# A hybrid diffusion trunk on one core: the first output group of each feed-forward chunk accumulates in four PSUM banks, and six modulation groups of TensorE stand at other places

## The chip, the cores and the metric

One NeuronCore of a Trainium2 chip runs the whole step as one program. The metric is the device time of that program in microseconds (us), the median of repeated executions; lower is better.

## The reference, cut to what matters

Two layers work on 640 tokens (512 latent, 128 context) of width 1024, in float32. Each layer is rmsnorm and half-step SwiGLU, rmsnorm and token mixing, rmsnorm and half-step SwiGLU. The norms are modulated by vectors that come from a conditioning vector through a wide matrix (`ada_w`).

```python
mod = (jax.nn.silu(cond) @ ada_w[i] + ada_b[i]).reshape(-1, N_MOD, D_MODEL)
h = modulate(rms_norm(x, norm_g[i, 0]), mod[:, 0], mod[:, 1])
x = x + 0.5 * mod[:, 2] * swiglu(h, ffn_w_in[i, 0], ffn_w_out[i, 0])
...
def swiglu(h, w_in, w_out):
    g, u = jnp.split(h @ w_in, 2, axis=-1)
    return (jax.nn.silu(g) * u) @ w_out          # inner width 2816 = 22 x 128
```

There are four feed-forward blocks, called F1 to F4 here (layer 0 first and last, layer 1 first and last).

## The kernel before, in words

**Layout.** Activations lie transposed: a tile is 128 channels by 640 tokens, and `x` is eight of them. A matmul takes a 128x128 weight tile as its stationary operand and half of the tokens, 320 columns, as its moving operand; `hf` names the half. Each float32 product is three matmuls of rounded operands (`mm3x`, lines 695 to 697): high by high, high weight by low activation, low weight by high activation. So every weight and every activation is split into a high part (a copy on ScalarE, `whi`, line 308) and a low part (a subtraction on VectorE, `wlo`, line 309).

**A feed-forward block.** Its 22 inner tiles are made in chunks of 6, 8 and 8 (`CHUNKS`), called c1, c2 and c3. For each inner tile `strassen_in` runs seven products into the three PSUM banks `pu`, `pg` and `pf`; ScalarE and VectorE then form the activation tile, first its high part (line 890), then its low part (line 891). Inner tiles are numbered 0 to 21; the trace names them `a`, layer, block, number (`a005h` is the high part of tile 5 of F1). After a chunk `out_proj` adds the chunk's share of the output to `x`: four weight groups (`fout`) of two output tiles, each for both token halves. One such output tile and half is a step (`op_step`): 3 matmuls for each inner tile of the chunk, in the order of the inner tiles, into one bank `op`; then VectorE adds the bank to `x` (`x_update`, line 807). The four groups of a chunk are called its section below. In c3 the x-update and the sums for the next norm have a raised priority (`tc.high_priority`), and its groups 2 and 3 run once for each half.

**Modulation groups.** Each group of 256 modulation channels (`ada`) is one load of 1 MB. Some run on TensorE (`ada`, line 447, into one bank `adaps` that is kept over four groups), the others as four long multiply-and-sum instructions on VectorE (`ada_v`, lines 404 and 406). In F1, F2 and F3 one VectorE group follows every `fout` group in the order of loads, and `mid_ada` starts it after the first step of that `fout` group. Twelve TensorE groups, six in F2 and six in F3, stand ahead of the inner tiles that `FA` lists.

**What sets the order.** All weights, `fout`, input weights and modulation groups alike, pass through a ring of two 1 MB slots (`raw`), in one written order (`order`), on SyncE's DMA queue. A weight's slot is free when its pieces are split, a modulation group's when its work is done. At most five split pieces are held; `splitter` splits ahead. TensorE's order in the feed-forward blocks and SyncE's order are those of the program text; VectorE's and ScalarE's are arranged by the compiler's scheduler, from priorities in the order of the text, and are then fixed. PSUM has eight banks (`psm`).

Of the kernel before, what the change touches and what calls it, by code (L numbers as in the profile page):

```python
# [32 lines left out]
SEGS = (((0, HT, 0),), ((HT, TL, 0), (TL, T, 1)))  # L33
NS = 47
NG0 = 2
FA = (4, 6, 9, 12, 14, 18)
QD_ = 512
NW = (6, 9)
HP = 60
# [28 lines left out]
def trunk_kernel(  # L68
# [55 lines left out]
    def stmp(name, dt=F32):  # L124
        return ap_.tile([P, T], dt, tag="s", bufs=NS, name=name)
# [5 lines left out]
    def psm(name):  # L131
        return pp.tile([P, 512], F32, tag="b", bufs=8, name=name)
# [18 lines left out]
    def spawn(gen, wait=0):  # L151
        e = [gen, wait]
        bgs.append(e)
        return e
# [57 lines left out]
    def ada_groups(l, mods):  # L212
        return [("ada", l, m * 4 + j) for m in mods for j in range(4)]

    def ffn_order(l, s):
        r, b = [], 0
        for ci, n in enumerate(CHUNKS):
            r += [("fin", l, s, g) for g in range(b, b + n)]
            r += [("fout", l, s, ci, g) for g in range(4)]
            b += n  # L220
        return r

    def weave(ws, ads, pads=(), fins=()):
        r, ads, pads = [], list(ads), list(pads)
        for w in ws:
            if pads and w[0] == "fin" and w[3] in fins:
                r.append(pads.pop(0))
            r.append(w)
            if ads and w[0] != "fin" and not (w[0] == "ein" and w[1] < 2):
                r.append(ads.pop(0))  # L230
        assert not ads and not pads
        return r

    order = [("ada", 0, m * 4 + j) for j in range(4) for m in (1, 0)]
    w00 = ffn_order(0, 0)
    q = 2 + sum(c in "ab" for c in SQ[:SQ.index("W")])
    order = order[:2] + w00[:1] + order[2:q] + w00[1:2] + order[q:]
    l1, pl = ada_groups(1, range(6)), ada_groups(1, range(6, 9))
    order += weave(w00[2:], ada_groups(0, [3, 4, 5]), ada_groups(0, [2]), (2, 3, 4, 5))
    order += weave([("ein", g) for g in range(10)] + [("eout", g) for g in range(4)], ada_groups(0, [6, 7, 8]))  # L240
    order += weave(ffn_order(0, 1), l1[:12], pl[:6], FA)
    order += weave(ffn_order(1, 0), l1[12:], pl[6:], FA)
    order += [("oin", g) for g in OORD] + [("oout", c, g) for c in range(2) for g in range(2)]
# [128 lines left out]
    def next_ada():  # L372
        if adae[0] is not None:
            finish(adae[0])
        k = order[st["i"]]
        adae[0] = spawn((ada_v if k[1:] in ADV else ada)(k))
        step(adae[0])

    def mid_ada():
        if st["i"] < nord and order[st["i"]][0] == "ada" and order[st["i"]][1:] in ADV:  # L380
            next_ada()

    def next_group(key):
        while order[st["i"]][0] == "ada":
            next_ada()
        j = st["i"]
        assert order[j] == key, (order[j], key)
        st["i"] += 1
        return Wt(j)
# [124 lines left out]
    def norm_acc(i, hf, k):  # L514
        t0, t1 = HALVES[hf]
        n = t1 - t0
        if (i, hf) not in nacc:
            acc = stmp(f"nq{i}{hf}")
            nacc[i, hf] = acc
            S.activation(out=acc[:, :n], in_=x[k][:, t0:t1], func=AF.Square)  # L520
        else:
            acc = nacc[i, hf]
            q = stmp(f"nq{i}{hf}{k}")
            S.activation(out=q[:, :n], in_=x[k][:, t0:t1], func=AF.Square)  # L524
            if k == KD - 1 and i == len(PHASES):
                nlast[i, hf] = q
            else:
                V.tensor_tensor(out=acc[:, :n], in0=acc[:, :n], in1=q[:, :n], op=ALU.add)  # L528
# [153 lines left out]

    def mm3(o, W, mcol, k, act, hf, start, stop):
        wh, wl = W.col(k, mcol)
        mm3x(o, wh, wl, *halves(act, hf), start, stop)

    def halves(act, hf):
        if len(act) == 2:
            t0, t1 = HALVES[hf]
            return act[0][:, t0:t1], act[1][:, t0:t1]  # L690
        return act[2 * hf], act[2 * hf + 1]

    def mm3x(o, wh, wl, xh, xl, start, stop, more=False):
        o = o[:, 0:HT]
        PE.matmul(o, wh, xh, start=start, stop=False, skip_group_check=more)  # L695
        PE.matmul(o, wh, xl, start=False, stop=False, skip_group_check=more)  # L696
        PE.matmul(o, wl, xh, start=False, stop=stop, skip_group_check=more)  # L697
        tick()

    def mm_fm(o, W, mcol, acts, hf, ks=None):  # L700
        ks = list(range(len(acts))) if ks is None else ks
        for i, k in enumerate(ks):
            mm3(o, W, mcol, k, acts[k], hf, i == 0, i == len(ks) - 1)

    def first_wide(i, keys, names):
# [6 lines left out]

        def go(a, k, W, hfs):
            for hf in hfs:
                for j in range(2):
                    mm3(ps[a, j, hf], W, j, k, h[k], hf, k == 0, k == KD - 1)
# [87 lines left out]
    def x_update(ps, m, l, gmod, hf):  # L804
        t0 = HALVES[hf][0]
        for a, b, c in SEGS[hf]:
            V.scalar_tensor_tensor(out=x[m][:, a:b], in0=ps[:, a - t0:b - t0],  # L807
                                   scalar=mod[:, l, gmod * KD + m, c:c + 1], in1=x[m][:, a:b],
                                   op0=ALU.mult, op1=ALU.add)

    def out_proj(keys, acts, l, gmod, nxt, ks=None):
        nw = len(keys) if nxt is None else 2
        for gi in range(nw):
            W = next_group(keys[gi])
            for j in range(2):
                for hf in range(2):
                    op_step(keys[gi], W, gi, j, hf, acts, l, gmod, nxt, ks)
                    mid_ada()
            W.done()
        if nw == len(keys):  # L820
            return
        la[0] = 2
        Ws = {}
        end = nxt == len(PHASES)
        for n_, hf in enumerate((1, 0) if end else (0, 1)):
            pe_manual((n_ == 1 or keys[0][0] == "fout") and not end)
            for gi in (2, 3):
                if n_ == 0:
                    Ws[gi] = next_group(keys[gi])
                for j in range(2):  # L830
                    op_step(keys[gi], Ws[gi], gi, j, hf, acts, l, gmod, nxt, ks)
                    mid_ada()
                if n_ == 1:
                    Ws[gi].done()
            chains[nxt, hf] = spawn(norm_chain(nxt, hf, NW[hf]))

    def op_step(key, W, gi, j, hf, acts, l, gmod, nxt, ks):
        ps = psm("op" + "_".join(str(v) for v in key[1:]) + f"_{j}{hf}")
        mm_fm(ps, W, j, acts, hf, ks)
        if nxt is None:  # L840
            x_update(ps, 2 * gi + j, l, gmod, hf)
        else:
            with tc.high_priority(HP):
                x_update(ps, 2 * gi + j, l, gmod, hf)
                norm_acc(nxt, hf, 2 * gi + j)

    def strassen_in(i, l, s, g, e):
        ahi, alo, sg = e
# [654 lines left out]
    ps = psm("n0p")  # L1503
# [4 lines left out]
    m = tiny([P, 5], "n0m")  # L1508
# [147 lines left out]
```

## Time and profile before

| | us |
|---|---|
| median of 3 runs | 2505.2 |
| lowest, highest | 2503.99, 2509.65 |
| the profiled execution, its own time | 2501.56 |
| its span in the profile | 2499.8 |

TensorE's mean granted clock over the span is 0.982 of full speed. The profiled execution lies a little below the runs; 1.8 us of it lie outside of the span.

### The profile page before, as it was taken

How to read it: one execution, taken by the hardware profiler on the slowest of the kernel's cores; microseconds unless marked ns; L12 is line 12 of the kernel's file. 1: busy time of each engine (PE TensorE's matmuls, PEld its weight loads, DVE VectorE, ACT ScalarE, POOL GpSimd, SP SyncE). 2: the span in 40 equal slices, each digit the busy share in tenths (PEclk: the TensorE clock that was granted, in tenths of full speed). 3: DMA queues.
4: the chain of work that ended last, by engine and by line, in shares of the span. 5: the costliest groups of instructions: out<-in, count | busy, mean ns of one | idle time of the engine just before them, and what ended most of it. 6: DMA issues, size and time to landing. Idle time of an engine off the chain costs nothing.

```text
span 2499.8 us, 40660 instructions
## 1 busy us (share of the span) xinstructions
PE 2398.9 (96%) x16482; PEld 2341.4 (94%) x16482; DVE 1863.5 (75%) x3785; ACT 1077.8 (43%) x2038; POOL 62.6 (3%) x86
## 2 busy tenths in 40 slices
PE   7899999999899999999999999999999998999998
PEld 6899999899898999999988999999999988999998
DVE  7677767877878777677967786789788877574674
ACT  4525335333326335153542433526767645252452
POOL 1000000000000000000000000001011000000000
PEclk9999999999999999999999999999999999999999
DMA  7342423323241333423224242342111101222121
GB/s 265 114 156 85 150 70 116 135 104 131 71 150 53 129 122 122 152 101 119 85 93 144 102 169 88 116 163 80 41 43 57 54 34 60 76 85 101 68 102 42
DMA packets 44475, 259.30 MB, mean 104 GB/s; under 512 B 5888, under 2 KB 8576, under 8 KB 16768
## 3 DMA queue, kind: packets, MB, share of 16 engines
q1 hardware_dynamic: 41024, 252.37, 28.4%
q8 instruction: 129, 2.11, 0.3%
q0 software_dynamic: 1280, 2.62, 0.3%
q10 hardware_dynamic: 1984, 1.72, 0.2%
q14 instruction: 58, 0.48, 0.1%
HBM read 252.76 MB, written 3.93 MB: 103 GB/s over the span
## 4 chain that ended last, share of the span: by engine, by line
PE 79%; DVE 11%; ACT 3%; DMA 3%; issue 2%; POOL 0%; POOLq 0%; ACTq 0%; DVEq 0%
PE op L696 7%; PE op L697 7%; PE op L695 7%; PE pu L695 7%; PE pu L696 7%; PE pu L697 7%; PE pg L697 4%; PE pg L696 4%; PE pg L695 3%; DVE wlo L309 3%; PE pf L695 2%; PE pf L696 2%; PE pf L697 2%; ACT whi L308 2%; DMA raw<-in_w_fout 1%
## 5 line engine op out<-in xcount | busy, mean ns | idle before, releaser
L309 DVE TENSOR_TENSOR wlo<-raw,whi 128x1024 fp32r<-128x1024 f32 (+1 forms) x488 | 536.1, 1116 | 282.5 <-ACT whi L308 281.4
L308 ACT ACTIVATE whi<-raw 128x1024 fp32r<-128x1024 f32 (+1 forms) x492 | 471.0, 974 | 632.5 <-DMA raw<-in_w_fout 147.8
L807 DVE SCALAR_TENSOR_TENSOR xs<-op,mod,xs 128x128 f32<-128x128 f32 (+2 forms) x312 | 127.1, 436 | 136.9 <-PE op L697 136.5
L524 ACT ACTIVATE nq<-xs 128x320 f32<-128x320 f32 x84 | 39.1, 468 | 132.2 <-DVE xs L807 130.6
L404 DVE SCALAR_TENSOR_TENSOR raw<-raw,sb 128x1024 f32<-128x1024 f32 x72 | 87.6, 1222 | 0.5
L406 DVE CUSTOM_DVE_ANT_0 raw<-raw,sb 128x1024 f32<-128x1024 f32 x72 | 87.5, 1219 | 0.7
L695 PE MATMUL oq<-H4h,whi 128*128 128x320 f32 x256 | 81.1, 318 | 0.2 <-ACT ov L967 0.2
L697 PE MATMUL oq<-H4h,wlo 128*128 128x320 f32 x256 | 79.6, 311 | 0.0
L696 PE MATMUL oq<-H4l,whi 128*128 128x320 f32 x256 | 79.3, 310 | 0.0
L1304 DVE TENSOR_REDUCE amx<-as 128x1 f32<-128x320 f32 x144 | 61.6, 461 | 19.1 <-PE as L1300 18.8
L1312 ACT ACTIVATE ap<-as,anm 128x320 f32<-128x320 f32 x128 | 66.1, 530 | 14.1 <-DVE anm L1307 13.9
L871 ACT COPY p<-pg 128x320 f32<-128x320 f32 x80 | 34.1, 426 | 64.0 <-PE pg L697 63.9
L291 DVE TENSOR_TENSOR raw<-raw 128x512 f32<-128x512 f32 x80 | 55.2, 690 | 1.9
L289 DVE TENSOR_TENSOR raw<-raw 128x512 f32<-128x512 f32 x80 | 55.2, 689 | 1.8
L290 DVE TENSOR_TENSOR raw<-raw 128x512 f32<-128x512 f32 x80 | 54.8, 685 | 0.8
L292 DVE TENSOR_TENSOR raw<-raw 128x512 f32<-128x512 f32 x80 | 54.8, 685 | 0.6
L695 PEld LDWEIGHTS oq<-H4h,whi 128*128 128x128 f32 x256 | 48.1, 188 | 1.3 <-ACT ov L967 0.5
L696 PEld LDWEIGHTS oq<-H4l,whi 128*128 128x128 f32 x256 | 48.1, 188 | 0.4 <-DVE H4l L614 0.3
L697 PEld LDWEIGHTS oq<-H4h,wlo 128*128 128x128 f32 x256 | 48.1, 188 | 0.0
L528 DVE TENSOR_TENSOR nq<-nq,nq 128x320 f32<-128x320 f32 x82 | 40.1, 491 | 9.6 <-ACT nq L524 9.1
L696 PE MATMUL pf<-H3p,whi 128*128 128x320 f32 x144 | 45.4, 316 | 1.8 <-DVE H3p L614 1.8
L696 PE MATMUL pf<-H5p,whi 128*128 128x320 f32 x144 | 44.8, 311 | 2.0 <-DVE H5p L614 2.0
(2715 smaller groups left out, 8899.2 us busy)
## 6 DMA issues: line engine op xcount, KB each, us to landing
raw<-in_w_fin SPq DMA_DIRECT2D x88, 1024.0 KB, 4.7
raw<-in_ada_w SPq DMA_DIRECT2D x64, 1024.0 KB, 4.7
raw<-in_w_fout SPq DMA_DIRECT2D x32, 1024.0 KB, 4.8
raw<-in_w_fout SPq DMA_DIRECT2D x16, 768.0 KB, 4.1
raw<-in_w_oin SPq DMA_DIRECT2D x12, 1024.0 KB, 4.8
raw<-in_w_ein SPq DMA_DIRECT2D x10, 1024.0 KB, 4.9
raw<-in_ada_w SPq DMA_DIRECT2D x32, 256.0 KB, 6.9
raw<-in_w_eout SPq DMA_DIRECT2D x4, 1024.0 KB, 4.9
```

The source lines that it names most:

```text
L289: sub.tensor_tensor(out=a22, in0=a21, in1=a22, op=ALU.add)
L291: sub.tensor_tensor(out=a11, in0=a22, in1=a11, op=ALU.subtract)
L308: S.activation(out=hf, in_=t, func=AF.Copy)
L309: sub.tensor_tensor(out=lf, in0=t, in1=hf.bitcast(F32), op=ALU.subtract)
L404: V.scalar_tensor_tensor(out=o, in0=w, scalar=1.0, in1=sb[:, c * D:(c + 1) * D], op0=ALU.mult, op1=ALU.mult, accum_out=r)
L406: V.tensor_tensor_reduce(out=o, in0=w, in1=sb[:, c * D:(c + 1) * D], scale=1.0, scalar=0.0, op0=ALU.mult, op1=ALU.add, accum_out=r)
L695: PE.matmul(o, wh, xh, start=start, stop=False, skip_group_check=more)
L696: PE.matmul(o, wh, xl, start=False, stop=False, skip_group_check=more)
L697: PE.matmul(o, wl, xh, start=False, stop=stop, skip_group_check=more)
L807: V.scalar_tensor_tensor(out=x[m][:, a:b], in0=ps[:, a - t0:b - t0], scalar=mod[:, l, gmod * KD + m, c:c + 1], in1=x[m][:, a:b], op0=ALU.m ...
L1304: V.tensor_reduce(out=mx[:, j, a:a + 1], in_=sps[j][a][:, 0:w], axis=AX.X, op=ALU.max, negate=True)
L1312: S.activation(out=pj[j][:, a * 320:a * 320 + w], in_=sps[j][a][:, 0:w], func=AF.Exp, bias=b, accum_out=(sm[:, j, a:a + 1] if full else s2 ...
```

## The change

Two edits. `FA` becomes (4, 8, 10, 12, 16, 18): of the six inner tiles that a TensorE modulation group precedes, tile 6 becomes 8, 9 becomes 10 and 14 becomes 16. And the first `fout` group of every chunk goes through the new function `op_wide` in place of four calls of `op_step`: it opens four banks, one for each output tile and half, and goes through the inner tiles in three cuts: all but the last two for each of the four banks, then the last but one for each of the four, then the last for each of the four with the x-update after each. `mid_ada` is called once, after the second cut. The x-update part of `op_step` becomes a function, `op_end`.

```diff
-FA = (4, 6, 9, 12, 14, 18)
+FA = (4, 8, 10, 12, 16, 18)
...
             W = next_group(keys[gi])
+            if gi == 0 and keys[0][0] == "fout":
+                op_wide(keys[0], W, acts, l, gmod, nxt)
+                continue
             for j in range(2):
                 for hf in range(2):
                     op_step(keys[gi], W, gi, j, hf, acts, l, gmod, nxt, ks)
                     mid_ada()
...
+    def op_wide(key, W, acts, l, gmod, nxt):
+        n = len(acts)
+        cuts = ((0, n - 2), (n - 2, n - 1), (n - 1, n))
+        jh = [(j, hf) for j in range(2) for hf in range(2)]
+        ps = {}
+        for c, (a, b) in enumerate(cuts):
+            for j, hf in jh:
+                if c == 0:
+                    ps[j, hf] = psm("op" + "_".join(str(v) for v in key[1:]) + f"_{j}{hf}")
+                for k in range(a, b):
+                    mm3(ps[j, hf], W, j, k, acts[k], hf, k == 0, k == n - 1)
+                if c == 2:
+                    op_end(ps[j, hf], j, hf, l, gmod, nxt)
+            if c == 1:
+                mid_ada()
+        W.done()
+
     def op_step(key, W, gi, j, hf, acts, l, gmod, nxt, ks):
         ps = psm("op" + "_".join(str(v) for v in key[1:]) + f"_{j}{hf}")
         mm_fm(ps, W, j, acts, hf, ks)
+        op_end(ps, 2 * gi + j, hf, l, gmod, nxt)
+
+    def op_end(ps, m, hf, l, gmod, nxt):
         if nxt is None:
-            x_update(ps, 2 * gi + j, l, gmod, hf)
+            x_update(ps, m, l, gmod, hf)
         else:
             with tc.high_priority(HP):
-                x_update(ps, 2 * gi + j, l, gmod, hf)
-                norm_acc(nxt, hf, 2 * gi + j)
+                x_update(ps, m, l, gmod, hf)
+                norm_acc(nxt, hf, m)
```

## Rows read from the trace of the kernel before

**Rows 1.** The page's first part: busy time, share of the span and number of instructions of each engine.

```profile
PE 2398.9 (96%) x16482; PEld 2341.4 (94%) x16482; DVE 1863.5 (75%) x3785; ACT 1077.8 (43%) x2038; POOL 62.6 (3%) x86
```

**Rows 2.** The timeline of TensorE at the end of the first step of F1's c1 (start in us, duration, engine, line, what is written from what; in brackets the idle time before and what ended it).

```profile
136.34 0.31 PE L697 MATMUL op<-a004h,wlo 128*128 128x320 f32 x1
137.63 0.41 PE L695 MATMUL op<-a005h,whi 128*128 128x320 f32 x1 [0.98 <-ACT a005h L890]
...
138.74 0.30 PE L697 MATMUL op<-a005h,wlo 128*128 128x320 f32 x1
```

**Rows 3.** The waits of TensorE over the whole span for parts of inner tiles: who waited for whom, idle us in total, times, longest.

```profile
PE op L695 <- ACT a105h L890: 1.4, 1, 1.4
PE op L696 <- DVE a0013l L891: 1.1, 1, 1.1
PE op L696 <- DVE a0021l L891: 1.1, 1, 1.1
...
PE op L696 <- DVE a0121l L891: 1.1, 1, 1.1
PE op L695 <- ACT a0013h L890: 1.1, 1, 1.1
PE op L696 <- DVE a1013l L891: 1.1, 1, 1.1
...
PE op L695 <- ACT a015h L890: 1.0, 1, 1.0
...
PE op L696 <- DVE a0113l L891: 1.0, 1, 1.0
PE op L696 <- DVE a1021l L891: 1.0, 1, 1.0
PE op L695 <- ACT a005h L890: 1.0, 1, 1.0
...
PE op L696 <- DVE a015l L891: 0.4, 1, 0.4
PE op L696 <- DVE a105l L891: 0.4, 1, 0.4
PE op L696 <- DVE a005l L891: 0.4, 1, 0.4
```

**Rows 4.** Stretches of the span: from and to in us, length, then busy us and number of instructions of PE, PEld, DVE, ACT and POOL, TensorE's granted clock as a share of full speed, share of the DMA engines' time, GB/s. The first follows the wait of F2's c1, the second lies behind that section of F3, the third is in the input projection of the odd layer.

```profile
848.30:851.70 3.40, 3.40 (x15) 3.40 (x14) 3.37 (x8) 0.00 (x0) 0.00 (x0) 0.50 0.30 125
...
1360.30:1367.10 6.80, 6.38 (x23) 5.94 (x24) 4.07 (x6) 2.33 (x4) 0.00 (x0) 0.50 0.44 154
...
1686.00:1692.00 6.00, 5.98 (x43) 5.72 (x42) 5.42 (x24) 3.07 (x5) 0.00 (x0) 1.00 0.37 156
```

**Rows 5.** The timeline of TensorE where F2's and F3's c2 begins, at inner tile 6: the modulation group's matmuls (`adaps`), then the products `pu`, `pg` and `pu` again, twelve matmuls each.

```profile
889.00 1.07 PE L447 MATMUL adaps<-raw,sc 128*32 128x256 f32 x16
890.00 0.41 PE L695 MATMUL pu<-H2p,whi 128*128 128x320 f32 x1
...
894.63 0.42 PE L695 MATMUL pg<-T20ah,whi 128*128 128x320 f32 x1 [2.62 <-ACT whi L308]
...
895.89 0.50 PE L697 MATMUL pg<-T20ah,wlo 128*128 128x320 f32 x1 [0.70 <-DVE wlo L309]
...
898.59 0.47 PE L695 MATMUL pu<-T20bh,whi 128*128 128x320 f32 x1
...
1355.44 0.42 PE L695 MATMUL pu<-H3p,whi 128*128 128x320 f32 x1
...
1364.45 0.47 PE L695 MATMUL pu<-T30bh,whi 128*128 128x320 f32 x1
```

**Rows 6.** The loads and splits behind that, from the timelines of SyncE's queue, ScalarE, VectorE and TensorE: first in F1, where no TensorE modulation group stands ahead of tile 6, then in F2, last the queue in F3.

```profile
162.52 0.33 SPq L267 DMA_DIRECT2D raw<-in_w_fin  x1
...
169.72 1.58 ACT L308 ACTIVATE whi<-raw 128x1024 fp32r<-128x1024 f32 x2 [10.34 <-DMA raw<-in_w_fin]
...
179.28 3.49 DVE L309 TENSOR_TENSOR wlo<-raw,whi 128x1024 fp32r<-128x1024 f32 x3
...
180.55 0.41 PE L697 MATMUL pg<-T00ah,wlo 128*128 128x320 f32 x1
...
872.95 0.33 SPq L264 DMA_DIRECT2D raw<-in_ada_w  x1
...
882.90 0.33 SPq L267 DMA_DIRECT2D raw<-in_w_fin  x1
...
887.75 1.58 ACT L308 ACTIVATE whi<-raw 128x1024 fp32r<-128x1024 f32 x2 [17.96 <-DMA raw<-in_w_fin]
...
1338.39 0.33 SPq L264 DMA_DIRECT2D raw<-in_ada_w  x1
```

**Rows 7.** Timelines in the sections: the first instruction of the second VectorE modulation group in F2's c2 and in F2's c3; in F2's c3 the first low piece of the last `fout` group, and the matmul that needs it; in F1's c3 the matmul that needs the last `fout` group.

```profile
1005.62 1.23 DVE L406 CUSTOM_DVE_ANT_0 adaj<-raw,sb 128x1024 bf16<-128x1024 f32 x1
...
1176.08 1.21 DVE L406 CUSTOM_DVE_ANT_0 adaj<-raw,sb 128x1024 bf16<-128x1024 f32 x1
...
1188.04 1.22 DVE L309 TENSOR_TENSOR wlo<-raw,whi 128x1024 fp32r<-128x1024 f32 x1 [0.68 <-ACT whi L308]
...
1192.49 0.31 PE L695 MATMUL op<-a0114h,whi 128*128 128x320 f32 x1
...
474.09 0.41 PE L695 MATMUL op<-a0014h,whi 128*128 128x320 f32 x1 [2.57 <-ACT whi L308]
```

## Prediction, made before the changed kernel ran

> **What bounds the kernel now.** I read the page's first part first [rows 1]: TensorE is busy for 2398.9 of 2499.8 us. In an engine so full only its idle time and its clock can be won by a change of order, so the views that matter are those of its waits and of its granted clock; VectorE, busy for 75%, is second and feeds it. Next, the waits of TensorE, kept to those that the two edits touch, and one of them in the timeline, to learn what a wait really costs. In F1's c1 the last matmul ahead of the wait starts at 136.34 and the third after it at 138.74 [rows 2]. A matmul follows the one before by 0.147 us when nothing is late (twelve take 1.76), so these three steps should take 0.44 and took 2.40: 1.96 lost, where the view shows 1.0 + 0.4 idle [rows 3]. Each such wait costs its idle time and some 0.27 more, in which the pipe drains and fills. Then the granted clock by stretches: behind the wait of F2's c1 it is 0.50, the lower of its two levels (1.2 of 2.4 GHz), for 3.4 us [rows 4], which costs 1.7 us more; behind F1's, as long, it did not fall. Last, what the late operand waited for, followed back through ScalarE, VectorE and the load queue [rows 6].
>
> **Part 1: the wide first group.** It removes no matmul and adds none. What it moves is the place at which the chunk's last tile is needed. The section of F1's c1 begins 14 matmuls before 136.34, at 134.29, and its first step wants tile 5 after 15 matmuls, 2.2 us; the low part is there by about 138.4. With four banks, 48 matmuls come before the last tile but one and 60 before the last: 7.0 and 8.8 us (10.5 and 12.3 in c2 and c3). So the parts, late by 2 us now, would be early by 4 or more, and I see nothing that would hold a tile back so long: its instructions stand ahead of the section's other work in the text. What this is worth, from [rows 3] with 0.27 for each wait:
> - c1: F1 1.0 + 0.4 + 0.54 = 2.0; F2 the same and 1.7 for the clock = 3.6; F3 1.4 + 0.4 + 0.54 = 2.4.
> - c2: F1 1.1 + 1.1 + 0.54 = 2.7; F2 1.0 + 0.27 = 1.3; F3 1.1 + 0.27 = 1.4.
> - c3: 1.4, 1.4 and 1.3.
> - F4 has no VectorE modulation groups in its sections and hardly waits: nothing.
>
> That is 17.5 us at the most. Bank pressure costs nothing: four banks, the last tile's three and `adaps` are eight, and the three are read before the last tile exists, so they are free long before group 1 asks for a bank. The four x-updates now come together; VectorE has the time of group 1's first step, 2.6 us or more, before anything else of TensorE's ends.
>
> Interleaving banks is something the kernel does already: the input projections change bank after every three matmuls. In one such stretch the granted clock is 1.00 and TensorE has no gap [rows 4], so I cost it at nothing. The Trainium skill ("TensorE: Matmul & The Clock Gate", section "A second HAM failure mode: psum-queue depth-cycling") says otherwise for a kernel that cycles its PSUM queue through banks: TensorE idles a little at each group of matmuls, and its clock swings between the two levels. By it the forecast would become rival 4's time; by the row it stays.
>
> **Part 2: `FA`.** A TensorE modulation group ahead of tile 6 takes a ring slot between the last modulation group of c1's section and tile 6's weights. In F2 that slot is filled at 872.95, and tile 6's own load starts only at 882.90, when the VectorE group ahead has finished; it lands at 887.7 [rows 6], and `pg`, the first product that needs the combined weights, waits for high part and low part. From 890.00 to 898.59 TensorE does 24 matmuls, 3.5 us of work, so 5.1 us are lost, and the clock is still low for some time: 5.4. In F3, 1355.44 to 1364.45, it is 5.5, and the clock stays at 0.50 to 1367.10 [rows 4, 5], 1.1 more after what two transposes rightly take: 6.6. With the group moved to tile 8, tile 6 gets the slot of 872.95. The moved group's own matmuls (1.0 us, row of 889.00) are paid at 8 instead: no change. I cost 9 to 10, 14 to 16 and 8 itself at nothing: in mid-chunk the load has a whole tile's time (84 matmuls, 12.3 us), and the present places 9, 12 and 18 show no wait. Without that cover 8 would cost what 6 does.
>
> **What is late next.** Both edits take time out of TensorE's side, and then the loads and VectorE set the pace. This is the working that cuts 29.5 us (17.5 and 12.0) down.
> - *F1, c1.* No TensorE group stands ahead of tile 6 there, and still its combined low piece is ready at 179.28 + 1.2 = 180.5 and its matmul starts at 180.55 [rows 6]: just in time, at a pace with 2.0 us of waiting in it. The chain behind (splits, modulation groups, loads) starts with the section and doesn't wait for TensorE. So most of the 2.0 comes back as a wait here: 0.5 gained, bounds 0 and 2.0.
> - *F2, c1.* TensorE would begin tile 6 at 890.00 - 1.0 - 3.6 = 885.4 and want the combined piece 14 matmuls later, at 887.5. A load issued a little behind another takes 7.2 us (162.52 to 169.72), so tile 6 lands at 880.1. From landing to that piece it takes 10.8 us in F1 (to 180.5), with a VectorE group between, and 8.1 in F2 (887.75 to 895.89); the mean, 9.4, gives 889.5. Wait: 2.0, and 0.7 for two chances in five that the clock falls. Gain 3.6 + 5.4 - 2.7 = 6.3, bounds 4 and 9.
> - *F3, c1.* By the same steps: wanted at 1355.44 - 1.0 - 2.4 + 2.05 = 1354.1, ready at 1338.39 + 7.2 + 9.4 = 1355.0. Gain 2.4 + 6.6 - 0.9 - 0.7 = 7.4, bounds 5 and 9.
> - *c2.* The next chunk's first pieces are split long ahead and held by the limit of five. I keep 5.0 of 5.4.
> - *c3.* `mid_ada` now stands after 84 of group 0's 96 matmuls instead of after 24, some 8.8 us later. Behind the waiting VectorE group in the queue are the loads of `fout` groups 2 and 3. In c1 and c2 the scheduler pulls modulation groups far ahead of their place in the text (F2's c2 starts the second one 8.4 us into its section), but in c3 it doesn't (1176.08, 20.1 us into it) [rows 7]. There a later start is really later. Slack of the last `fout` group in F2: its first low piece ends at 1189.3, it is wanted at 1192.49: 3.2 us, of which the removed wait takes 1.4. In F1's c3 there is none: TensorE waits already at 474.09, so nothing of its 1.4 is won and any delay is lost. Bounds: all 4.1 won, or a wait of F1's kind new in each: 2.57 + 0.27, less what is won, and a fall of the clock, some 4 each, so -12. I take -2.5, nearer the gain, since the slack covers most of the delay: F1 -1.5, F2 and F3 -0.5 each.
>
> Sum: 0.5 + 6.3 + 7.4 + 5.0 - 2.5 = **16.7 us**. The span goes from 2499.8 to 2483.1, the profiled execution from 2501.56 to 2484.9. That execution was 3.6 us under the median; against the median it is 2505.2 - 16.7 = **2488.5 us**.
>
> **Rivals.**
> 1. *Everything is won.* VectorE, with no x-updates during the first 8.8 us of a section, does its modulation groups sooner and nothing is given back: 29.5 us, 2475.7. For it: the idle VectorE there. Against: F1's tile 6, just in time.
> 2. *c3 is late.* The three third sections end at -12: 16.7 - 9.5 = 7.2 gained, 2498.0. For it: 1176.08 and 474.09 [rows 7].
> 3. *The other side: every section is late.* If VectorE keeps the modulation groups where the text has them in all nine sections, `fout` groups 2 and 3 come late in each, at the 2.84 of 474.09 and 1.7 for the clock, 4.5: 19.2 (the sum without c3) less 40.5 is 21.3 lost, 2526.5. It decides from 2.1 us a section on. Against it: 1005.62, far ahead of the text.
> 4. *The clock swings while banks alternate.* 24 matmuls of the second and third cut in 12 sections at 0.267 instead of 0.147 us are 34.6 us: 2523.1. Against it: the third of [rows 4]. The skill's rule named above is this one; no trace here bears it out so far.
> 5. *The wait is moved, not removed.* Tile 8 becomes what tile 6 was: the 12.0 of `FA` stay, 4.7 gained, 2500.5. Against: places 9 and 12.
>
> **How the numbers follow.** Forecast 0.58 (its own range 2481 to 2495, the bounds of c1 and c3 partly set against each other), rival 1 0.13, rival 2 0.15, rival 3 0.05, rival 4 0.02, rival 5 0.07. About 0.2%, 5 us, is what a measurement can tell from no change. Faster are the forecast, rival 1 and most of rival 2: 0.82. Same are rival 5 and the rest of rival 2: 0.11. Slower are rivals 3 and 4: 0.07. The range goes from rival 1 to the far end of rival 2, 2475 to 2503; it leaves out rivals 3 and 4 and about half of the spread around rival 1, some 0.14.
>
> **What would show it.** Right: no wait of `op` for a last tile in F1 to F3; `adaps` at tile 8, and tile 6's load about 10 us earlier in F2 and F3; waits of 0 to 3 us at the first `pg` of tile 6 in all three; no fall of the clock in c1's section of F2. Wrong: new waits of `op` for weights (`whi`, `wlo`) in groups 2 and 3, first in c3; waits at tile 8; a granted clock of 0.50 in the first groups; VectorE starting the first modulation group 12 us into a section of c1 or c2.

## The result, and the profile after

The changed kernel takes 2489.4 us (median, 2488.8 to 2490.2) against 2504.6 us (2501.8 to 2509.7) for the kernel before: a ratio of 0.9939, 95% interval 0.9926 to 0.9953, 15.2 us. A second measurement of it (experiment 5) gave 0.9924 (0.9905 to 0.9942). The forecast was 2488.5 us. Of the changed kernel there are two profiled executions, spans 2487.7 and 2488.6 us, 12.1 and 11.2 less than before. They are called the first and the second trace here; that they differ inside is a main result below.

The page's first part (first trace), which answers to [rows 1]:

```profile
PE 2395.3 (96%) x16482; PEld 2339.5 (94%) x16482; DVE 1858.1 (75%) x3785; ACT 1076.8 (43%) x2038; POOL 63.0 (3%) x86
```

TensorE's waits, first trace (who waited for whom, idle us in total, times, longest; over the whole span, so waits in stages without an edit are in the totals). The waits for inner tiles of [rows 3] are gone; what is left of `op`, `pu` and `pg` waits for weights or for a bank that ScalarE or VectorE has to read:

```profile
PE pg L697 <- DVE wlo L309: 10.3, 8, 2.7
PE pg L695 <- ACT whi L308: 9.3, 6, 2.4
...
PE op L695 <- ACT whi L308: 3.4, 2, 3.2
```

Where those behind the two edits stand, in TensorE's timeline (first trace): tile 6 of F1, the last `fout` group but one of F1's c3, tile 6 of F2, tile 6 of F3, then tiles 8 and 15 of F3. In brackets the idle time and its releaser:

```profile
179.64 0.42 PE L695 MATMUL pg<-T00ah,whi 128*128 128x320 f32 x1 [1.47 <-ACT whi L308]
...
180.90 0.41 PE L697 MATMUL pg<-T00ah,wlo 128*128 128x320 f32 x1 [0.70 <-DVE wlo L309]
...
465.43 0.64 PE L695 MATMUL op<-a0014h,whi 128*128 128x320 f32 x1 [3.18 <-ACT whi L308]
...
888.76 0.42 PE L695 MATMUL pg<-T20ah,whi 128*128 128x320 f32 x1 [1.47 <-ACT whi L308]
...
890.02 0.42 PE L697 MATMUL pg<-T20ah,wlo 128*128 128x320 f32 x1 [0.70 <-DVE wlo L309]
...
1347.61 0.41 PE L695 MATMUL pg<-T30ah,whi 128*128 128x320 f32 x1 [2.43 <-ACT whi L308]
...
1348.87 0.64 PE L697 MATMUL pg<-T30ah,wlo 128*128 128x320 f32 x1 [0.71 <-DVE wlo L309]
...
1383.66 0.42 PE L695 MATMUL pu<-T30ah,whi 128*128 128x320 f32 x1 [2.00 <-ACT a108s L897]
...
1534.24 0.41 PE L695 MATMUL pu<-T30bh,whi 128*128 128x320 f32 x1 [1.30 <-DVE p L904]
```

Windows of the first trace (columns as in [rows 4]): the wide group of F2's c1, first cut and then the cuts that alternate between four banks every three matmuls; the stretch behind the waits of F1's tile 6; the one behind 465.43.

```profile
843.00:850.00 7.00, 7.00 (x49) 7.00 (x49) 5.83 (x9) 1.95 (x4) 0.00 (x0) 1.00 0.41 150
850.00:853.60 3.60, 3.60 (x27) 3.60 (x26) 3.54 (x7) 0.00 (x0) 0.00 (x0) 1.00 0.02 5
...
181.40:184.80 3.40, 3.40 (x15) 3.40 (x14) 1.72 (x2) 0.51 (x2) 0.00 (x0) 0.50 0.53 159
...
464.70:471.60 6.90, 5.81 (x20) 5.41 (x21) 2.82 (x5) 1.62 (x2) 0.00 (x0) 0.51 0.84 292
```

The granted clock is 1.00 through the wide group and TensorE has no gap in it. So rival 4 is out: the clock doesn't swing while the banks alternate. The section of the Trainium skill that the prediction named for it ("TensorE: Matmul & The Clock Gate", "A second HAM failure mode: psum-queue depth-cycling") describes another kernel's case; this trace doesn't show it.

The span term by term. Each is measured from the start of a section to the start of the next stage that the prediction charged it to (the c1 terms from the start of c1's section to that of c2's, and so on; the c3 terms cover the section alone, and F4's holds its first chunk and the end of the span); + is time won:

```
term                     predicted   first trace   second trace
F1 c1                       +0.5        -2.2          -0.7
F2 c1                       +6.3        +5.9          +5.0
F3 c1                       +7.4        +1.3          +5.8
c2 (F1, F2, F3)             +5.0        +3.4          +5.0
c3 (F1, F2, F3)             -2.5        +1.4          -0.6
F4, sections and chunks      0          +1.3          +0.4
stages without an edit       0          +1.0          -3.7
sum                        +16.7       +12.1         +11.2
```

### The profile page after: what moved, and what is told of

It is laid out like the page before. It is cut to its first block, busy times and chain, and to the rows that moved or that the text cites. A ratio compares the mean times of both kernels' runs of the same rounds, so it can differ in the third digit from the quotient of the medians.

```text
span 2487.7 us, 40652 instructions
## 1 busy us (share of the span) xinstructions
PE 2395.3 (96%) x16482; PEld 2339.5 (94%) x16482; DVE 1858.1 (75%) x3785; ACT 1076.8 (43%) x2038; POOL 63.0 (3%) x86
## 4 chain that ended last, share of the span: by engine, by line
PE 80%; DVE 11%; ACT 3%; DMA 2%; issue 2%; POOL 0%; POOLq 0%; ACTq 0%; DVEq 0%
PE op L695 8%; PE op L697 8%; PE op L696 8%; PE pu L695 7%; PE pu L696 7%; PE pu L697 7%; PE pg L697 4%; PE pg L696 4%; PE pg L695 3%; DVE wlo L309 3%; PE pf L695 2%; PE pf L696 2%; PE pf L697 2%; PE oq L695 1%; PE atb L1378 1%
## 5 line engine op out<-in xcount | busy, mean ns | idle before, releaser
L1327 DVE TENSOR_REDUCE amx<-as 128x1 f32<-128x320 f32 x144 | 61.5, 460 | 19.1 <-PE as L1323 18.8
L1335 ACT ACTIVATE ap<-as,anm 128x320 f32<-128x320 f32 x128 | 66.2, 531 | 14.1 <-DVE anm L1330 13.9
L696 PE MATMUL pf<-H2p,whi 128*128 128x320 f32 x144 | 44.6, 311 | 1.8 <-DVE H2p L614 1.8
```

The source lines that it names most:

```text
L1327: V.tensor_reduce(out=mx[:, j, a:a + 1], in_=sps[j][a][:, 0:w], axis=AX.X, op=ALU.max, negate=True)
L1335: S.activation(out=pj[j][:, a * 320:a * 320 + w], in_=sps[j][a][:, 0:w], func=AF.Exp, bias=b, accum_out=(sm[:, j, a:a + 1] if full else s2 ...
```

## The experiments

All were timed against the kernel before, runs of one group on the same chip (1 to 4, 5 to 8, 9 to 12). Diffs are against the changed kernel.

**1 and 2. Each edit alone.** The wide group with the old `FA`, and the new `FA` with the old first group:

```diff
-FA = (4, 8, 10, 12, 16, 18)
+FA = (4, 6, 9, 12, 14, 18)
```
```diff
-            if gi == 0 and keys[0][0] == "fout":
-                op_wide(keys[0], W, acts, l, gmod, nxt)
-                continue
```

> The wide first group with the old FA. Theory A (the chain of loads and splits behind a first section starts with that section and does not wait for TensorE, so time won in c1 comes back as a longer wait at tile 6 as long as a TensorE modulation group stands there): c1 gives nothing in F2 and F3 and loses 2 in F1; c2 gives 4 to 5 us, c3 of F2 and F3 2.7, c3 of F1 loses 1.3. Together 4 to 5 us faster than before, about 2500; the wait of pg at tile 6 grows from 2.6 to 4 us or more of idle time in F2. Rival B (each edit takes away its own waits, and the two add up): 3.6 and 2.4 more are kept, about 10 us faster than before, about 2494.5, and tile 6 waits as before.

> The new FA with the old first group. Theory A: TensorE comes to tile 6 later by what it still waits for (3.6 us in F2, 2.4 in F3), the pieces are ready by then, so nearly all of 5.4 and 6.6 us is won, less up to 4 us if the new waits at tiles 8 and 15 of F3 come with FA: 8 to 12 us faster than before, 2493 to 2497; at tile 6 of F2 and F3 hardly any wait. Rival B (adding up): 15.2 less what the wide group alone gives, some 5 us faster, about 2500.

Measured: wide group alone 2490.4 us, ratio 0.9942 (0.9930 to 0.9955); new places alone 2490.7, 0.9945 (0.9932 to 0.9958). Both are better than either theory said, and the two gains, 13.9 and 13.6, don't add to 15.2. The stages that were expected do behave as theory A has it. With the wide group alone F2's c1 wins 1.4 of 3.6 and F3's 0.5 of 2.4 (in the second profile of this kernel, experiment 11, they lose 1.8 and 0.1), since TensorE, earlier at tile 6, now waits there twice (timeline of that kernel):

```profile
889.03 0.42 PE L695 MATMUL pu<-H2p,whi 128*128 128x320 f32 x1 [2.12 <-ACT whi L308]
...
890.29 0.42 PE L697 MATMUL pu<-H2p,wlo 128*128 128x320 f32 x1 [0.70 <-DVE wlo L309]
...
894.22 0.64 PE L695 MATMUL pg<-T20ah,whi 128*128 128x320 f32 x1 [1.84 <-ACT whi L308]
...
895.47 0.64 PE L697 MATMUL pg<-T20ah,wlo 128*128 128x320 f32 x1 [0.36 <-DVE wlo L309]
```

With the new places alone there is no wait at tile 6, and F2's and F3's c1 win 5.5 and 3.8. Much of the rest of both gains lies where no edit is: F3's first chunk is 3.6 us shorter with the wide group alone and 3.0 with the new places alone, F4's first chunk 2.5 in the former. Experiments 11 and 12 return to it.

**3. The modulation call earlier, and 4. F1's c1 in four single steps.**

```diff
-            if c == 1:
-                mid_ada()
+                if c == 0 and (j, hf) == (0, 0):
+                    mid_ada()
```
```diff
-            if gi == 0 and keys[0][0] == "fout":
+            if gi == 0 and keys[0][0] == "fout" and keys[0][1:4] != (0, 0, 0):
```

> The changed kernel, but the VectorE modulation group of the first output group is started after the first of the four banks of the first cut (as many steps from the start as before) instead of after the second cut. Theory C (the later start is what made F1's c3 worse: its first modulation group ran 15.9 us into the section, 5.6 before): the wait in F1's c3 goes back to group 3 and from 7.5 to about 5 us; c1 and c2 stay; 2 us faster than the changed kernel, about 2487.5. Rival (the scheduler arranges VectorE's work by data and priority, and the tables of the mixer come first in either case): no change, 2489.5 within 1 us, and the group in F1's c3 still starts 12 us or more into the section.

> The changed kernel with the old first group in F1's c1 alone. Theory A: the 2.0 us of waiting for the last tile are back, the 4.2 us at tile 6 (wait and lower clock) are gone: 2 us faster than the changed kernel, about 2487.3. Rival B: only the 2.0 are back, about 2491.4, and tile 6 of F1 waits as in the changed kernel.

Measured: 2487.6 us, ratio 0.9930 (0.9917 to 0.9942), and 2486.4, 0.9924 (0.9909 to 0.9938). In F1's c3 VectorE's first modulation group starts at 440.35 in the kernel before and 449.80 in the changed one, 5.6 and 15.9 us into the section; with the earlier call 4.3. That section then takes 2.0 us less than before instead of 1.3 more, with a short wait and no fall of the clock (timeline of kernel 3):

```profile
437.32 1.22 DVE L404 SCALAR_TENSOR_TENSOR adaj<-raw,sb 128x1024 bf16<-128x1024 f32 x1
...
470.07 0.41 PE L695 MATMUL op<-a0014h,whi 128*128 128x320 f32 x1 [1.69 <-ACT whi L308]
```

In kernel 4 the wait of F1's tile 6 is gone: TensorE begins the tile at 178.06 instead of 176.25 and `pg` at 179.82 with no wait, and F1's c2 section starts at 276.75, where the changed kernel has 279.05 (277.42 in its second trace) and the one before 277.15. Both theories hold.

**5. The changed kernel once more, and 6. edits 3 and 4 together.**

> The changed kernel, unchanged, once more. Both theories expect 2489.4 us for the time. It is run for what its second trace shows of single stretches. If the stretches that no edit touches (the first chunks of F3 and F4, where the low clock took 13.6 us in one profile and 6.8 in another) belong to an order of instructions, they come out within 0.5 us of the first trace of this kernel. If they differ from execution to execution (the rival), they come out up to 4 us apart, with the low clock falling at other places. The waits at tile 6 of F1, F2 and F3 (idle 2.2, 2.5 and 3.1 us) should be there again within 0.3 us under both, for they come from the order of the loads; the load ahead of tile 6 of F3, 8.7 us from issue to landing in the first trace, tells whether 8.7 is that place's own time or an accident.

> Two of the edits run before, together: the modulation call after the first bank of the wide group's first cut, and F1's c1 with its first group in four single steps. The theory, that the two act in different sections (F1's c3, and F1's tile 6) and so add: 2489.4 less 1.9 less 3.0 is 2484.5 us, F1's c2 section starting 0.4 us earlier than in the kernel before and F1's c3 section losing about 2 where the changed kernel loses 7.5. The rival, that what one part wins is taken back by the loads, as wide group and places of the TensorE groups did (14.1 and 13.9 us singly, 15.2 together): 2486.4, no better than the better of the two.

Measured: 2488.0 us, 0.9924 (0.9905 to 0.9942); edits 3 and 4 together 2484.0, 0.9908 (0.9889 to 0.9927), near the 2484.5 of the theory that they add, though the intervals overlap. In the trace F1's sections and chunks end 5.5 us earlier than in the first trace.

The second trace answers where the first was odd. Its stages without an edit come out between the two theories: F3's and F4's first chunk, whose instructions stand in the same order, are 0.9 and 0.5 us longer than in the first trace. The waits at tile 6 are there again, 1.47 and 0.70 in each of F1, F2 and F3, but in F1 the clock does not fall behind them, so F1's c1 loses 0.7 and not 2.2. In F2 it is the other way round: no fall in the first trace, one in the second, and 5.0 us won for 5.9 (windows of the second trace, behind the waits of F1 and F2):

```profile
180.80:184.20 3.40, 3.39 (x23) 3.39 (x24) 2.23 (x2) 1.02 (x3) 0.00 (x0) 1.00 0.39 82
892.60:896.00 3.40, 3.40 (x15) 3.40 (x14) 1.15 (x2) 0.43 (x1) 0.00 (x0) 0.50 0.70 231
```

In F3 it is the load of tile 6 that differs. From issue to the start of the split it took 8.8 us in the first trace and 7.5 in the second, and at tile 8, where a modulation group's load follows behind, 7.5 and 5.5 (SyncE's queue and ScalarE; first trace, then second):

```profile
1329.93 0.33 SPq L267 DMA_DIRECT2D raw<-in_w_fin  x1
...
1338.70 1.58 ACT L308 ACTIVATE whi<-raw 128x1024 fp32r<-128x1024 f32 x2 [12.33 <-DMA raw<-in_w_fin]
...
1374.27 0.33 SPq L267 DMA_DIRECT2D raw<-in_w_fin  x1
1376.54 0.33 SPq L264 DMA_DIRECT2D raw<-in_ada_w  x1
...
1381.72 1.58 ACT L308 ACTIVATE whi<-raw 128x1024 fp32r<-128x1024 f32 x2 [3.33 <-DMA raw<-in_w_fin]
1383.20 0.41 ACT L897 COPY a108s<-pu 128x320 f32<-128x320 f32 x1
```
```profile
1333.36 0.33 SPq L267 DMA_DIRECT2D raw<-in_w_fin  x1
...
1340.88 1.58 ACT L308 ACTIVATE whi<-raw 128x1024 fp32r<-128x1024 f32 x2 [10.65 <-DMA raw<-in_w_fin]
...
1375.24 0.33 SPq L267 DMA_DIRECT2D raw<-in_w_fin  x1
...
1380.69 1.58 ACT L308 ACTIVATE whi<-raw 128x1024 fp32r<-128x1024 f32 x2 [1.33 <-DMA raw<-in_w_fin]
1382.17 0.41 ACT L897 COPY a108s<-pu 128x320 f32<-128x320 f32 x1
```

At tile 8 ScalarE's copy of `pu`, which frees the bank, stands behind the split of the next weights in its queue; with that load 2.0 us quicker TensorE doesn't wait there at all. A wait of this kind of over 0.5 us stands in nine other places of the traces, 1.0 to 2.0 us long, each at a tile that a TensorE modulation group precedes: F3's tile 8 in kernels 2, 4 and 6, F3's tile 4 in kernels 4, 6 and 7 and in the second trace, F3's tile 11 in kernel 8, and F2's tile 9 in kernel 11. So F3's c1 term has a spread of its own: 1.3 and 5.8 us in the two traces, 4.5, 0.9, 1.9 and 1.4 in those of kernels 3, 4, 6 and 8, which have the same c1 there but for the place of the call or of the TensorE group.

**7. The VectorE modulation group ahead of tile 6 put behind it.**

```diff
             r.append(w)
-            if ads and w[0] != "fin" and not (w[0] == "ein" and w[1] < 2):
+            if ads and w[0] == "fin" and w[3] == CHUNKS[0]:
+                r.append(ads.pop(0))
+            if ads and w[0] != "fin" and not (w[0] == "ein" and w[1] < 2) and not (w[0] == "fout" and w[3:] == (0, 3)):
                 r.append(ads.pop(0))
```

> The changed kernel with one thing moved in the order of the weights: the VectorE modulation group that stands behind the last output group of c1, ahead of tile 6's weights, comes behind tile 6 instead (in F1, F2 and F3). Theory: what is late at tile 6 is its load, which waits for the ring slot that this modulation group holds; so with the group behind it the waits for whi and wlo at tile 6 (idle 2.2, 2.5 and 3.1 us and 0.54 for each pair, with a fall of the clock in F1 and F3) are gone, and F1's, F2's and F3's c2 sections start some 3, 2.5 and 4 us earlier than in the changed kernel: about 2480 us, 2476 to 2484. Rival: the chain of loads has no slack at all, and the group that is moved makes tile 7 or 8 late by as much: the waits turn up there, and the time stays at 2487 to 2491.

Measured: 2501.3 us, 0.9979 (0.9968 to 0.9990), worse than both numbers, but by the rival's mechanism. The waits at tile 6 are gone. In F2, tile 8 now has two modulation groups in the ring ahead of its weights, and the wait comes there, 6.1 us idle instead of 2.2 (timeline):

```profile
917.54 0.52 PE L697 MATMUL pu<-H2p,whi 128*128 128x320 f32 x1 [3.47 <-ACT whi L310]
...
918.80 0.64 PE L699 MATMUL pu<-H2p,wlo 128*128 128x320 f32 x1 [0.48 <-DVE wlo L311]
...
923.04 0.41 PE L697 MATMUL pg<-T20ah,whi 128*128 128x320 f32 x1 [1.47 <-ACT whi L310]
...
924.30 0.46 PE L699 MATMUL pg<-T20ah,wlo 128*128 128x320 f32 x1 [0.70 <-DVE wlo L311]
```

F3 does the same at 1381.79, and in F1, with no TensorE group near, tile 7 waits 1.08 and 0.89 at 203.86. Behind c1 the chain has no slack to move a wait into.

**8. `FA` with 9, 11 and 13 in place of 8, 10 and 12.**

```diff
-FA = (4, 8, 10, 12, 16, 18)
+FA = (4, 9, 11, 13, 16, 18)
```

> The changed kernel with the TensorE modulation groups ahead of tiles 4, 9, 11, 13, 16 and 18 in place of 4, 8, 10, 12, 16 and 18. Theory: the wait at tile 8 of F3 (idle 2.0 us, ScalarE's copy standing behind the split of the next weights, whose load went out beside that of the modulation group) is a cost of the place 8; with 9 it is gone and F3's c1 and c2 win 2.3 us more: about 2487 us. Rival: the wait at tile 8 comes from the late weights of tile 6 in F3, whatever group stands at 8, or goes with the group to tile 9: 2489.4 us, no change. Tile 6 itself should be as in the changed kernel under both.

Measured: 2489.8 us, 0.9932 (0.9915 to 0.9949): no change. The waits at tiles 8 and 15 of F3 are absent, but the second trace of the changed kernel, run beside it, has no wait there either, so their absence shows nothing about the place; and a wait of the same kind, 1.19 us, comes at tile 11 (1426.34), where a group now stands. Tile 6 of F3 waits 2.02 and 0.36, and the clock falls behind it. The time is the rival's; the question of the place isn't settled by it.

**9. Half of one modulation group left out.**

```diff
                 r = mod[:, l, 2 * g + m, c:c + 1]
+                if c == 1 and (l, g) in ((0, 15), (1, 3), (1, 15)):
+                    V.tensor_copy(out=r, in_=mod[:, l, 2 * g + m, 0:1])
+                    continue
```

> The changed kernel, with half of VectorE's work left out in one modulation group of each of F1, F2 and F3: the fourth group of c1, which stands ahead of tile 6's weights, works out one of its two conditions (two of four instructions, some 2.5 us less) and copies the other, so the output is not the reference's. Nothing else moves. Theory: at tile 6 it is VectorE that is late, because it has this group and the pieces of tile 6 to do one behind the other; with 2.5 us less the waits at tile 6 (idle 2.2 us in F1 and F2, 2 to 3 in F3) shrink to under 0.7 or are gone, no clock falls there, and nothing new comes at tiles 7 and 8, since work is taken away and not moved: 1.5 to 3 us in each, about 2482 us where the changed kernel gave 2488.0 and 2489.4. Rival: the landing of the load sets the piece, whatever VectorE does: the waits stay within 0.4 us and the time at 2487 to 2490.

Measured: 2473.9 us, ratio 0.9876 (0.9860 to 0.9891), 8 us below the theory's time. At tile 6 nothing is left but one short wait for the low part in each of F1, F2 and F3, with no fall of the clock there:

```profile
179.30 0.41 PE L700 MATMUL pg<-T00ah,wlo 128*128 128x320 f32 x1 [0.45 <-DVE wlo L309]
...
886.47 0.41 PE L700 MATMUL pg<-T20ah,wlo 128*128 128x320 f32 x1 [0.45 <-DVE wlo L309]
...
1338.92 0.41 PE L700 MATMUL pg<-T30ah,wlo 128*128 128x320 f32 x1 [0.70 <-DVE wlo L309]
```

The three c1 terms are +1.4, +8.4 and +7.4, against -0.7, +5.0 and +5.8 in the second trace: 7.0 us more, which is what the theory asked for. Another 6.9 us against that trace lie in the first chunks of F3 and F4, which are short here as in kernel 1; that part the theory didn't foresee (experiments 11 and 12). The landing doesn't decide as long as it isn't very late: tile 6's load in F3 took 7.6 us here too, and in the two traces of the changed kernel the last wait at tile 6 ends 46.9 us into the section in all five places where that load landed after 6.1 to 7.4 us, and at 47.9 in the sixth, where it took 8.7.

It also shows how the half group does it. In F3 the group's ring slot is free 7.5 us after its load went out (1321.54 to 1328.99, when tile 7's load goes out); in the first trace it took 14.0 (1328.79 to 1342.77). There the group's fourth instruction stood on VectorE behind a low piece of tile 6, and that piece waited for tile 6's load (first trace):

```profile
1339.79 1.23 DVE L309 TENSOR_TENSOR wlo<-raw,whi 128x1024 fp32r<-128x1024 f32 x1 [2.11 <-ACT whi L308]
...
1341.52 1.22 DVE L406 CUSTOM_DVE_ANT_0 raw<-raw,sb 128x1024 f32<-128x1024 f32 x1
...
1342.77 0.33 SPq L267 DMA_DIRECT2D raw<-in_w_fin  x1
```

But more than VectorE's work changed, so the cause isn't shown to be VectorE's alone. ScalarE's order at tile 6 is turned over as well: its copy of `pu` (`a006s` in F1) waits for TensorE's first product of that tile. In the kernel before the three splits of the combined weights stand ahead of this copy in F1; in the changed kernel they stand behind it, in F1, F2 and F3, and as the copy waits for TensorE itself, their place in the section is the same in five of the six (F1, kernel before, then first trace):

```profile
177.42 2.96 ACT L308 ACTIVATE whi<-raw 128x1024 fp32r<-128x1024 f32 x3 [6.12 <-DVE raw L291]
180.44 0.43 ACT L867 COPY a006s<-pu 128x320 f32<-128x320 f32 x1
```
```profile
178.21 0.43 ACT L890 COPY a006s<-pu 128x320 f32<-128x320 f32 x1 [7.48 <-PE pu L697]
178.53 2.95 ACT L308 ACTIVATE whi<-raw 128x1024 fp32r<-128x1024 f32 x3
```

In kernel 9 they stand ahead again, as they do wherever c1 has single steps and no TensorE group precedes tile 6 (kernels 2, 4, 6, 10 and 12). VectorE had the weights for the first of these splits combined at 177.72 in the first trace (line 291, 0.68 us from 177.04), so an estimate from these rows gives the order up to 0.8 us of F1's wait of 2.2, and VectorE the rest; in the second trace it is 0.4, and in F3 of the first, where VectorE is last, nothing. An exchanged order alone was not run.

**10. The wide group in c2 and c3 alone**, with the earlier call of kernel 3:

```diff
-            if gi == 0 and keys[0][0] == "fout":
+            if gi == 0 and keys[0][0] == "fout" and keys[0][3] > 0:
```

> The wide group in c2 and c3 alone (c1 of every block in four single steps), the modulation call after the first bank of its first cut, the new places of the TensorE groups. It tells what the wide group is worth in c1. Theory: nothing, for what it wins there the chain of loads and VectorE takes back at tile 6. So F2's c1 and F3's c1 win what the new places alone won (5.5 and 3.8 us), there is no wait at tile 6, and the time is that of the kernel with wide groups in c1 of F2 and F3 as well, 2484.0 us, within 1.5. Rival: the terms of the prediction for c1 (3.6 and 2.4 us with the fall of the clock) are won in part also with the wait behind: then this kernel is 3 us slower or more, 2487 to 2489.

Measured: 2482.4 us, 0.9909 (0.9889 to 0.9929), against 0.9908 of kernel 6. The times favour the theory, but with intervals of 5 us to either side they can't exclude the rival's 3 us; the traces do better. F2's and F3's c1 win 5.5 and 6.6 us, with no wait at tile 6. In the three profiles with single steps there (kernels 2, 10 and 12) they win 5.5 to 7.2 and 3.8 to 6.6, in the six with the wide group (the two traces, kernels 3, 4, 6 and 8) 4.9 to 6.3 and 0.9 to 5.8. So on top of the new places no gain of the wide group shows in c1; what it wins there is waited for again. This and kernel 6 have the lowest ratios of those that compute everything, but their intervals overlap that of the changed kernel, so a gain over it isn't settled.

**11 and 12. Each edit alone, again.**

> The wide group alone with the old places, once more. In its first profile the sections that the edit touches gained 7.9 us together and stages that it doesn't touch 4.5 (F3's first chunk 3.6, F4's 2.5). Theory: those 4.5 belong to that execution, and the time of the kernel stays where it was measured, 2490.4 us within 1.5, while the stages of the trace come out differently: F3's first chunk within 1 us of the kernel before. Rival: they belong to this order of instructions, and F3's first chunk is 3 us or more shorter again.

> The new places alone with the old first group, once more. In its first profile F2's c1 gained 5.5 us, F3's c1 3.8, and F3's first chunk, which no edit touches, 3.0. Theory: the first two come again within 1 us, with no wait at tile 6, and F3's first chunk is within 1 us of the kernel before; the time is 2490.7 us within 1.5. Rival: the gain of F3's first chunk belongs to the edit and is there again, 2.5 us or more.

Measured: 2492.2 us, 0.9944 (0.9930 to 0.9959), and 2495.9, 0.9962 (0.9948 to 0.9976), 0.3 and 3.7 us beyond the theories' bounds. With the new places alone F2's and F3's c1 win 7.2 and 4.2 us, again with no wait at tile 6. The rival is right on the stages: F3's first chunk is shorter again, by 3.8 and 3.7 us. It is so in five profiles, those of kernels 1, 2, 9, 11 and 12 (3.0 to 3.8), and in none of the other eight behind the change (from 0.3 shorter than before to 1.4 longer). VectorE's order there parts the kernels in the same way. Kernel 11 does `T33al` ahead of two low pieces; the changed kernel (second trace, in the second fence), and the kernel before, after them:

```profile
1254.77 0.83 DVE L509 TENSOR_TENSOR T32bl<-H3t,T32bh 128x640 fp32r<-128x640 f32 x1
1255.51 0.83 DVE L509 TENSOR_TENSOR T33al<-H3t,T33ah 128x640 fp32r<-128x640 f32 x1
1256.24 2.36 DVE L309 TENSOR_TENSOR wlo<-raw,whi 128x1024 fp32r<-128x1024 f32 x2
```
```profile
1248.68 2.35 DVE L309 TENSOR_TENSOR wlo<-raw,whi 128x1024 fp32r<-128x1024 f32 x2
...
1251.68 0.82 DVE L509 TENSOR_TENSOR T32bl<-H3t,T32bh 128x640 fp32r<-128x640 f32 x1
1252.42 0.82 DVE L509 TENSOR_TENSOR T33al<-H3t,T33ah 128x640 fp32r<-128x640 f32 x1
...
1253.29 0.63 PE L696 MATMUL pg<-T33al,whi 128*128 128x320 f32 x1 [2.71 <-DVE T33al L509]
```

The last line is the wait that it makes. Each edit alone tips the scheduler into the better order, and the two together back into the old one; the half group left out in kernel 9 tips it again. That is some 6 of the 12 us by which the single gains of 1 and 2 exceed the joint one (3.6 and 3.0, less 0.3 in the first trace); in F4's first chunk, 2.5 us shorter in 1, 9 and 11 alone, VectorE's order differs in just these three as well. That the order makes the time is inferred from this agreement; an exchanged order alone was not run.

The times of kernel 2 and 12, one and the same, are 5 us apart. In the trace of 12 the old first group waits longer than ever before, in F3's c2, where [rows 3] had 1.1:

```profile
1455.88 0.41 PE L695 MATMUL op<-a1013h,whi 128*128 128x320 f32 x1 [2.03 <-ACT a1013h L890]
1457.43 0.64 PE L696 MATMUL op<-a1013l,whi 128*128 128x320 f32 x1 [1.15 <-DVE a1013l L891]
```

With the fall of the clock it makes that section and chunk 5 us longer; F4 loses 4 in the same way. That execution, 2499.3 us, is the slowest of the six. No profile with the wide group in a section has a wait for an inner tile there, so it removes that source of spread, which one trace of before can't show. That its times spread less isn't shown: the six runs of kernel 6 lie 14 us apart, those of kernel 10 12.

## Why the prediction was right

- **What the waits cost.** Right. In c2, where nothing is late behind, the predicted 5.0 came as 5.0 in the second trace and 3.4 in the first; F1's c2 alone gave 2.74 for the 2.7 worked out from idle time and 0.27 for each wait; since kernels 2 and 12 take 0.8 and 0.9 less there without the wide group, part of it was the wait of that one trace. The first trace lost 1.6 (1.30 idle and 0.3) at tile 15 of F3.
- **Part 2.** Right: no long wait at tile 6 of F2, and F2's c1 won 5.9 and 5.0 where 6.3 was predicted. A wait of 2.0 was predicted; 2.2 us of idle time came, 2.7 with 0.27 for each of the two waits.
- **F1's c1.** That the time won comes back as a wait at tile 6 was right, as kernels 4 and 9 show; the size was not. The step took the low piece as ready at 180.5, because the chain behind "doesn't wait for TensorE". It came at 180.9, and counted from the start of the section 0.6 us later than before (46.9 for 46.3): ScalarE's splits now stood behind a copy that does wait for TensorE (experiment 9). The wait costs its idle time and twice 0.27, 2.7 us, more than the 2.0 won. That gives -0.7, as in the second trace; the first has a fall of the clock besides. The lower bound, 0, took the piece's time as fixed.
- **F3's c1.** The term that was mis-sized: 7.4 predicted, with bounds 5 and 9, and 1.3 and 5.8 measured. The step took 7.2 us for tile 6's load from a single row of F1; in F3 it took 7.4 to 8.7 in the traces of kernels with this c1. From there to the low piece's matmul it took 9.4, the mean of F1 and F2; 10.2 and 10.5 came (from 1338.70 to 1348.87, and in the second trace from 1340.88 to 1351.33), near the 10.8 of F1, where a VectorE group stood between as it now does in F3. So even the second trace waits 2.2 us idle and 0.5 for the two waits, where 0.9 was predicted, and with the load of 8.7 the wait grows by 1 us more. The clock falls behind it in all of these traces but the second one of the changed kernel; I had priced that at two chances in five. And the places in mid-chunk, costed "at nothing", did cost in the first trace: 2.3 us at tile 8, where a load landed 2 us later than in the second.
- **c3.** In F1 right: -1.5 predicted, -1.3 and -1.8 measured, and kernel 3 shows that the call's place is the cause. In F2 and F3, with -0.5 predicted for each, the sign was wrong in three of four: +1.4 in both traces of F2, +1.3 and -0.2 in F3. The step said that the scheduler doesn't pull the group ahead in c3. With the call moved it does: in F2 the first group of that section starts at 1153.07, 4.2 us into it, where the call itself stands some 12 us in, and the second at 1168.02, 19.1 us in, for 20.1 before [rows 7].
- **The total.** Within 1 us of the forecast by the median. In the traces the gain is 4.6 and 5.5 short of 16.7: in the first mostly by F3's c1, in the second mostly by stages without an edit. The medians gain 3 to 6 us more than these two spans, mostly because the profiled execution of before, 2501.6 us, was 3.0 under its median. The sum was good to about 5 us, and that it met the median so closely is partly luck.
- **Rivals.** Rival 1 (everything is won) is out: F1's c1 loses time by the wait at tile 6. Rivals 2 and 3 (late sections) are out: the three third sections together end at +1.4 and -0.6, and the second ones win. Rival 4 is out by the windows above. Rival 5 (the wait is moved) came true in the first trace's tile 8, at a fifth of its price of 12 us.

## What to carry to other kernels

Before counting a removed wait as won, follow the next operand that the same queue brings, and on every engine that it passes: here the c1 waits that the wide group removed came back at the next tile, and what moved that point was less work on VectorE (half a group, 7 us), in a run in which ScalarE's order changed with it. Put two traces of one kernel side by side before explaining a term of 2 to 5 us, and compare stage by stage, with the engines' order in stages without an edit: a list scheduler can turn them over too. Two edits measured singly needn't add: here they lean on the same chain, and about half of what is missing was an order turned over elsewhere.

## What the runs showed of the hardware

- A load of 1 MB in the same place of the same program took 7.5 us from issue to its first use in one execution and 8.8 in another (F3's tile 6, rows above).
- The same two waits, 1.47 and 0.70 us idle, were followed by 3.4 us at a granted clock of 0.50 in F1's tile 6 of the first trace, and by none in the second; in F2's tile 6 it was the second that had the fall. A fall can't be told from the length of the wait alone.
- TensorE's granted clock stays at 1.00 while it changes among four banks every three matmuls without a gap (850.00 to 853.60).
